# TensorE's issue order taken from the source in the whole program of a two-layer hybrid block

## The chip, the cores and the metric

The kernel runs on one core of one Trainium2 chip. The metric is the device time of one launch in microseconds (us), here the median of the runs shown. A core has TensorE (PE in the profile, its weight loads PEld), VectorE (DVE), ScalarE (ACT), GpSimd (POOL) and SyncE (SP), each with an instruction stream of its own that it works off in order; SP, ScalarE and GpSimd also issue DMAs. An engine waits on semaphores where an instruction needs a result of another engine.

## The reference

Input is `x` (1024 tokens of width 1024), a context of 256 tokens, two conditioning vectors, and the weights of two layers. Each layer does:

```
mod = silu(c) @ ada_w + ada_b                     # six vectors of 1024, for tokens and context
h   = rmsnorm(x) * (1 + scale) + shift            # the same for the context
u   = h @ w_in                                    # split over four mixers of width 256
y   = [rglru(u_a), hgrn2(u_b), ssd(u_s), mla(u_m)]
x   = x + gate * (concat(y) @ w_out)
x   = x + gate * expert_choice_ffn(modulate(rmsnorm(x)))   # 16 experts of width 512
```

`rglru` is a gated linear recurrence after a short convolution, `hgrn2` and `ssd` are chunked linear attentions run forward and backward, `mla` is softmax attention with low-rank projections over context and tokens. Each expert takes the 128 tokens (32 of the context) with the largest router weights for it. The context is carried on to layer 1 and is not updated by it. All is float32.

## The kernel before

**Emission.** Each stage of a layer is a Python generator: `ada` (the modulation vectors), `norm1`, `eproj`, `lru_x`, `lru_gate`, `ssd`, `ssd_chunk`, `ssd_z`, `hgrn_v`, `hgrn_g`, `hgrn_block`, `hgrn_group`, `hgrn_out`, `mla_prep`, `mla` with its `maxima`, `wout`, `route`, `experts`. `layer` (L2024) spawns them as threads, and `weave` (L223) resumes one thread after another, by simple clocks of the engines and by hand-set due times in the table `ORDER`, up to its next `yield`. So the instructions of the stages are emitted woven into one sequence: that is the order of the source. In it, a group of projection matmuls (`proj_ch`, `proj_tok`, in thirds or halves) stands between, say, two levels of a recurrence group.

**Issue.** The compiler does not keep that sequence. It plans each engine by a timing model of its own, takes the emission order as a priority, and lets a later instruction go first on an engine where by its plan the earlier one still lacks an operand or a buffer. It also hands out the buffers of the pools by its plan. The exception is the main part of `experts`, which stands in a region that fixes the order of every engine:

```
L1976        yield from self.wait(f"route{l}.0")
L1977        with self.tc.manual_schedule():
L1978            prep(0)
```

**Matmuls.** Projections split both operands into a high and a low part and make three passes (`ps<-A,W`, `ps<-W,A`, `ps<-C,A` in the profile). `A` holds the activations, `W` weights and small work tiles (7 buffers), `C` (10 buffers) weights and long rows, `M` (14 buffers) short tiles, `ps` the 8 PSUM banks. A plain float32 matmul appears as two records in the trace.

**Places that the prediction speaks of.**
- `ada`, L407: per step of 128 rows of `ada_w` two loads of 512 KB into `W` and four matmuls `ps<-W,sT` of 32 columns of weights. After the first block, which loads into `A`, it is a thread of layer 0 that makes the remaining vectors of both layers.
- `lru_x`, `proj_ch` (L552): projections of the recurrence `rglru`; the weight block is split by ScalarE and VectorE (L530) first.
- `hgrn_group`: level after level, scores (`scores`, L1044, tiles `ps<-C,M`) and, for the two largest levels, blocks added into one bank (L1097, `ps<-C,W`), with products on VectorE (L1100, L1102) between the levels. At most two groups are open at a time.
- `mla_prep`, `first` (L1249): transposes `ps<-cf,W` of a row tile that GpSimd has scaled.
- `ssd` L834 to 836, then `ssd_chunk` L868 and L870: the backward states are finished on VectorE one after another; the chunk's matmuls `ps<-C,C` read them, and the 512-column pair `ps<-W,cf` (L873, L874) follows.
- `place` (L1348): transposes `ps<-cf,M` of a row tile of queries or keys loaded from DRAM.
- `wout` (L1561): the output projection, `ps<-A,W` and `ps<-A,C`.

The profile puts nearly every instruction at L160, the helper through which all are recorded, so its rows are told apart by tiles.

Of the kernel before, what the change touches and what calls it, by code (L numbers as in the profile page):

```python
# [163 lines left out]
class Model:  # L164
# [1891 lines left out]
    def build(self):  # L2056
        self.mod = self.d([2, 2, 6144])
        self.prelude()
        for l in range(self.layers):
            self.layer(l)  # L2060
        if "y" in self.taps:
            for i, w in enumerate("lhs"):
                if w in self.which:
                    o = 0 if self.layers == 1 else 256
                    self.nc.sync.dma_start(self.taps["y"][256 * i:256 * i + 256, o:], self.yT[256 * i:256 * i + 256, o:])
        if "xc" in self.taps:
            self.nc.sync.dma_start(self.taps["xc"], self.xc)
            self.nc.sync.dma_start(self.taps["xl"], self.xl)
# [39 lines left out]
```

## Time and profile before

| | us |
|---|---|
| median of 3 runs | 2840.32 (2839.93 to 2845.86) |
| profiled execution | 2842.43 |
| its span, first to last instruction | 2840.6 |
| TensorE busy, weight loads busy | 2446.1 (86%), 1865.0 |
| VectorE, ScalarE, GpSimd busy | 1910.6, 1181.4, 910.9 |
| mean granted TensorE clock | 0.923 |

Layer 0 runs up to about 1570 us of the span, its expert stage from about 1100; layer 1 follows, with its expert stage from about 2490. Busy time is the time in which at least one instruction of the engine ran. In the rows of the timeline, a line merges neighbouring instructions of one kind: start, length, engine, operation, tiles, count, and in brackets the idle time before it with what ended it.

### The profile page before, as it was taken

The page shows a single profiled execution, that of the slowest core. Times are in us where ns is not written, and L with a number is a line of the kernel's source. Part 1 is how long each engine was busy: PE and PEld are TensorE (multiplying, and loading weights), DVE is VectorE, ACT ScalarE, POOL GpSimd, SP SyncE. Part 2 cuts the span into 40 slices and gives each one's busy share as a digit, 9 for nine tenths or more (in the row PEclk, how much of TensorE's full clock was granted, in tenths as well). Part 3 has the DMA queues.
Part 4 walks back from the last instruction along what each step waited for, and adds up shares of the span by engine and source line. Part 5 has one row for each costly group of instructions (what it writes and reads, how often), then busy time and mean ns, then how long its engine had stood idle before and what let it go on. Part 6 is the DMA issues. An engine that isn't in the chain of part 4 may idle for free. (4 is left out here: it accounts for less than half of the span.)

```text
span 2840.6 us, 50547 instructions
## 1 busy us (share of the span) xinstructions
PE 2446.1 (86%) x19427; PEld 1865.0 (66%) x19427; DVE 1910.6 (67%) x3894; ACT 1181.4 (42%) x2010; POOL 910.9 (32%) x930
## 2 busy tenths in 40 slices
PE   5879999988898794999999599799969989589888
PEld 3658888644554573777777588688746547367776
DVE  5445476566786646677887745753788764699996
ACT  3345223234343112555555352522353442266664
POOL 3112232242531113333333412322444312244443
PEclk8889999999999896999999899889979999789999
DMA  6222226468212433778888411133331034479996
GB/s 249 63 67 62 61 83 188 138 219 296 70 58 97 151 113 132 245 258 290 294 271 279 139 52 37 56 98 98 97 121 40 19 116 137 171 281 357 350 342 217
DMA packets 243440, 455.45 MB, mean 160 GB/s; under 512 B 25688, under 2 KB 155096, under 8 KB 242176
## 3 DMA queue, kind: packets, MB, share of 16 engines
q1 hardware_dynamic: 190176, 365.75, 37.2%
q0 software_dynamic: 12096, 37.75, 5.8%
q10 hardware_dynamic: 40928, 48.72, 4.9%
q8 instruction: 153, 2.51, 0.4%
q14 instruction: 87, 0.71, 0.1%
HBM read 377.55 MB, written 74.60 MB: 159 GB/s over the span
## 5 line engine op out<-in xcount | busy, mean ns | idle before, releaser
L160 PE MATMUL ps<-A,W 128*128 128x512 f32 (+3 forms) x4160 | 965.1, 379 | 34.4 <-ACT W L160 31.5
L160 PEld LDWEIGHTS ps<-A,W 128*128 128x128 f32 x4160 | 739.4, 195 | 179.6 <-ACT W L160 35.4
L160 DVE TENSOR_TENSOR A<-C,A 128x1024 fp32r<-128x1024 f32 x310 | 443.7, 1459 | 93.7 <-ACT A L160 87.4
L160 ACT ACTIVATE M<-ps 128x512 f32<-128x512 f32 (+6 forms) x576 | 262.3, 469 | 525.5 <-PE ps L160 444.3
L160 ACT ACTIVATE A<-C 128x1024 fp32r<-128x1024 f32 x384 | 392.0, 1058 | 187.9 <-DMA C<-in_moe_w_down_dram 64.5
L160 POOL TENSOR_TENSOR A<-C,A 128x1024 fp32r<-128x1024 f32 x74 | 208.0, 2815 | 214.6 <-ACT A L160 161.1
L160 PE MATMUL ps<-W,A 128*128 128x256 f32 x1344 | 192.5, 300 | 8.5 <-DVE A L160 7.4
L160 PE MATMUL ps<-A,M 128*128 128x512 f32 x768 | 186.7, 399 | 0.9 <-ACT M L160 0.9
L160 PEld LDWEIGHTS ps<-W,A 128*128 128x128 f32 x1344 | 177.0, 203 | 11.5 <-DVE A L160 8.1
L160 PE MATMUL ps<-cf,M 128*128 128x128 f32 (+3 forms) x416 | 74.4, 307 | 124.1 <-DVE M L160 89.3
L160 POOL TENSOR_TENSOR C<-C,M 128x512 f32<-128x512 f32 x76 | 110.2, 1461 | 193.9 <-ACT M L160 136.0
L160 PEld LDWEIGHTS ps<-A,M 128*128 128x128 f32 x768 | 142.8, 190 | 36.1 <-issue 3.1
L160 DVE TENSOR_TENSOR C<-C,M 128x512 f32<-128x512 f32 (+2 forms) x196 | 130.1, 676 | 40.7 <-ACT M L160 39.2
L160 PEld LDWEIGHTS ps<-cf,M 128*128 128x128 f32 (+2 forms) x416 | 53.6, 154 | 154.8 <-DVE M L160 74.9
L160 PE MATMUL ps<-C,A 128*32 128x128 f32 (+1 forms) x2528 | 148.0, 290 | 0.0
L160 PE MATMUL ps<-A 96*128 96x512 f32 (+3 forms) x368 | 132.9, 418 | 9.4 <-ACT A L160 4.0
L160 PEld LDWEIGHTS ps<-C,A 128*32 128x32 f32 (+1 forms) x2528 | 134.8, 127 | 6.9 <-issue 4.6
L160 ACT ACTIVATE W<-ps 128x512 fp32r<-128x512 f32 (+2 forms) x156 | 66.0, 476 | 174.8 <-PE ps L160 174.4
L160 PE MATMUL ps<-M,M 128*128 128x64 f32 (+3 forms) x968 | 116.8, 251 | 23.1 <-DVE M L160 12.6
L160 PE MATMUL ps<-A,C 128*128 128x512 f32 x352 | 134.2, 412 | 1.5 <-DVE C L160 1.4
L160 POOL TENSOR_TENSOR W<-W,C 128x512 f32<-128x512 f32 x33 | 49.6, 1521 | 256.9 <-DVE W L160 173.4
L160 ACT ACTIVATE C<-ps 128x512 f32<-128x512 f32 (+4 forms) x116 | 53.9, 469 | 177.8 <-PE ps L160 163.7
(239 smaller groups left out, 3906.7 us busy)
## 6 DMA issues: line engine op xcount, KB each, us to landing
C<-in_moe_w_gate_dram SPq DMA_DIRECT2D x128, 512.0 KB
C<-in_moe_w_up_dram SPq DMA_DIRECT2D x128, 512.0 KB
C<-in_moe_w_down_dram SPq DMA_DIRECT2D x128, 512.0 KB
W<-in_ada_w_dram SPq DMA_DIRECT2D x80, 512.0 KB
W<-in_w_in_dram SPq DMA_DIRECT2D x40, 512.0 KB
C<-dr SPq DMA_DIRECT2D x29, 512.0 KB
dr<-M ACTq DMA_DIRECT2D x114, 128.0 KB
M<-dr SPq DMA_DIRECT2D x46, 256.0 KB
```

Source lines behind the costliest of these rows:

```text
L160: return f(*args, **kw)
```

## The change

The loop over the two layers is put into a region that fixes the issue order of TensorE alone to the order of emission. VectorE, ScalarE, GpSimd and SP are left to the compiler as before, but for the region inside `experts`, which stays and now orders the engines that the outer one does not. `prelude` has no matmul, so every matmul of the program lies in the new region. No instruction, tile or operand is changed.

```
     def build(self):
         self.mod = self.d([2, 2, 6144])
         self.prelude()
-        for l in range(self.layers):
-            self.layer(l)
+        with self.tc.manual_schedule(engines={mybir.EngineType.PE}):
+            for l in range(self.layers):
+                self.layer(l)
```

## Rows read from the trace of the kernel before

**Rows 1.** The page, part 1: busy time, share of the span, instructions.
```profile
PE 2446.1 (86%) x19427; PEld 1865.0 (66%) x19427; DVE 1910.6 (67%) x3894; ACT 1181.4 (42%) x2010; POOL 910.9 (32%) x930
```

**Rows 2.** Busy time by window: length, busy (records) by engine, clock, DMA share, GB/s.
```profile
0.00:228.00 228.00, 168.67 (x961) 124.44 (x962) 108.92 (x188) 94.08 (x142) 59.78 (x72) 0.88 0.35 121
228.00:505.00 277.00, 259.83 (x4124) 235.02 (x4127) 164.06 (x435) 90.92 (x204) 70.96 (x109) 0.96 0.33 101
505.00:907.00 402.00, 362.86 (x1808) 209.00 (x1801) 286.36 (x682) 155.69 (x340) 141.78 (x209) 0.96 0.45 150
907.00:1100.00 193.00, 157.34 (x819) 120.60 (x819) 98.19 (x252) 42.85 (x93) 41.39 (x26) 0.85 0.42 139
1100.00:1570.00 470.00, 421.83 (x4087) 326.50 (x4087) 354.98 (x563) 242.23 (x300) 157.87 (x84) 0.94 0.77 255
1570.00:1985.00 415.00, 353.21 (x4141) 318.01 (x4142) 239.28 (x501) 160.54 (x306) 122.41 (x162) 0.91 0.26 79
1985.00:2350.00 365.00, 316.07 (x1498) 208.19 (x1497) 273.53 (x630) 146.73 (x306) 136.55 (x184) 0.92 0.25 81
...
2500.00:2840.60 340.60, 303.33 (x1444) 244.87 (x1442) 304.55 (x403) 212.59 (x248) 142.99 (x61) 0.96 0.91 318
```

**Rows 3.** Timeline of TensorE, 147 to 168 us, and SyncE's load at 161.
```profile
159.88 3.57 PE L160 MATMUL ps<-A,W 128*128 128x256 f32 x13 [10.99 <-ACT W L160]
163.38 1.37 PE L160 MATMUL ps<-W,sT 128*32 128x512 f32 x4
...
165.59 1.05 PE L160 MATMUL ps<-W,sT 128*32 128x512 f32 x4
...
161.12 0.34 SPq L403 DMA_DIRECT2D W<-in_ada_w_dram  x1
```

**Rows 4.** Timeline of TensorE, 228 to 236 us.
```profile
227.79 2.29 PE L160 MATMUL ps<-A,W 128*128 128x256 f32 x17
232.15 0.46 PE L160 MATMUL ps<-C,M 64*32 64x32 f32 x32 [2.06 <-ACT M L160]
...
233.92 2.36 PE L160 MATMUL ps<-A,W 128*128 128x256 f32 x9
```

**Rows 5.** Timeline of TensorE, 308 to 317 us.
```profile
308.12 1.84 PE L160 MATMUL ps<-W,A 128*128 128x256 f32 x13
311.20 0.62 PE L160 MATMUL ps<-C,W 64*32 64x32 f32 x48 [1.25 <-DVE C L160]
...
313.70 1.02 PE L160 MATMUL ps<-W,A 128*128 128x256 f32 x5
315.05 1.18 PE L160 MATMUL ps<-C,W 64*64 64x64 f32 x24 [0.33 <-DVE C L160]
```

**Rows 6.** Timeline of TensorE and VectorE, 2147.57 to 2154 us.
```profile
2147.57 1.66 PE L160 MATMUL ps<-C,C 64*128 64x128 f32 x9
...
2149.95 2.88 DVE L160 SCALAR_TENSOR_TENSOR C<-C,et 128x64 f32<-128x64 f32 x14
...
2152.03 0.49 PE L160 MATMUL ps<-C,C 64*128 64x128 f32 x4 [0.55 <-DVE C L160]
...
2152.88 0.49 PE L160 MATMUL ps<-C,C 64*128 64x128 f32 x4 [0.35 <-DVE C L160]
```

**Rows 7.** Timeline of TensorE, 2342.13 to 2343 us.
```profile
2342.13 0.63 PE L160 MATMUL ps<-A,W 128*128 128x512 f32 x1
2342.76 0.79 PE L160 MATMUL ps<-A,C 128*128 128x512 f32 x1
```

**Rows 8.** Busy time by window; columns as in rows 2.
```profile
232.30:235.70 3.40, 3.40 (x136) 3.33 (x129) 2.41 (x5) 3.37 (x4) 0.84 (x2) 0.50 0.22 64
```

**Rows 9.** Timeline of TensorE, 564 to 569 us.
```profile
565.35 1.15 PE L160 MATMUL ps<-W,sT 128*32 128x512 f32 x8
566.61 0.68 PE L160 MATMUL ps<-cf,W 128*128 128x128 f32 x3
```

**Rows 10.** Timeline of TensorE, 640 to 656 us.
```profile
652.17 2.77 PE L160 MATMUL ps<-cf,M 128*96 128x128 f32 x12 [4.34 <-DMA M<-dr]
```

## The prediction

> **What bounds the kernel now.** I read the page's first part, then busy time by stretch of the span, then TensorE's own timeline inside the stretches where it issues out of source order. TensorE is busy 86% of the span [rows 1]. By stretch [rows 2] it idles 59.3 us before 228 us, only 17.2 us of 277 between 228 and 505 (gated recurrence groups with projections between them), 39.1 of 402 up to 907 (state-space, attention preparation, attention), 35.7 up to 1100 (output projection, routing), and 48.2 and 37.3 in the two expert stretches. Layer 1 repeats this: 61.8 from 1570 to 1985, 48.9 up to 2350. So between 228 and 505 TensorE itself sets the pace, and elsewhere it often waits for others, who wait for it in turn.
>
> **Which instructions change place.** The program numbers its instructions in the order in which the source emits them, and the trace has them in the order of issue, so the two orders can be set side by side. Of 14,387 matmuls and transposes 2,369 stand elsewhere than in source order, in 56 closed stretches: 2 before 228, 13 from 228 to 505, 19 from there to 907, 3 to 1100, 12 from 1570 to 1985, 7 to 2350. No stretch lies in an expert stage: these stand in source order already, under their own region, so 470 and 340.6 us of the span stay. Nothing is added or removed: the same matmuls, the same bytes, the same work on the other engines. The one change is that where the compiler now lets a later matmul go first because an earlier one lacks its operand, TensorE will stand.
>
> **The cost of one stretch.** Take the state at which the compiler deviates, keep the recorded arrival of each operand, and lay the matmuls end to end in source order.
> - First stretch, 148.9 us [rows 3]. In the source four `ada` matmuls come first (each f32 matmul is two records) and 26 projections behind them. Now 13 projections start at 159.88 after 10.99 us of waiting, and `ada` is put in between, two by two. The second `ada` weight load is issued only at 161.12, so its two matmuls cannot run before about 161.5; they ran at 165.59. In source order all 26 projections stand behind that load: the stretch ends 0.4 us later (landing at 161.5) to 4.5 us later (at 165.6). I take +3.4, a landing near 164.5, nearer to the row in which the matmuls really ran.
> - 308.1 us [rows 5]. In the source 44 matmuls of the recurrence group (32 on tiles of 64*32 and 64*64, then 12 more of 64*64) stand ahead of 18 projections. Now 13 projections fill 308.12 to 309.96 and the group starts at 311.20 after 1.25 us; five more go at 313.70, ahead of the 12, which start at 315.05 after 0.33 us. In source order TensorE waits 311.20 - 308.12 = 3.08 and 315.05 - 313.70 = 1.35: +2.85 us net.
> - 2147.6 us, the largest [rows 6]. The first of the 64*128 matmuls in the source needs the last backward state, of which VectorE is making 14 pieces; it runs at 2152.88. In the source 11 others, the 512-column pair among them, stand behind it; now they start at 2147.57. TensorE would wait 2152.88 - 2147.57 = 5.3 us where it now loses 0.90 (0.55 + 0.35): +4.4.
> - Last stretch, 2342.1 us [rows 7]. One matmul of the output projection is pulled ahead of one that waits for VectorE until 2342.76: +0.6.
>
> The same sum for all 56 stretches, the first and the last of them above: +4.2, +16.5, +18.3, +2.6, +7.6, +7.9, in the order of the list, +57.1 us in all (only one stretch gains, 0.5). Were each operand's arrival fixed, a late TensorE would simply wait less at its next wait, and nearly all would be given back: the lower end is 0. Were each arrival to move with TensorE, all would stay: +57.
>
> Which? From 228 to 505 idle time is 17.2 us, about as much as the 16.5 to be added, and the recurrence is a ping-pong (a level's scores on TensorE, its products on VectorE, the next scores), so arrivals move with TensorE; but two groups are in flight, and a wait of one lets the other get ahead. I let two thirds stay: 11.0. Elsewhere 40.6 us are added beside 36 to 62 us of idle per stretch, so most is taken back: a quarter stays, 10.2.
>
> **The clock.** A wait can also cost after it has ended. At 232.15 TensorE starts again after 2.06 us [rows 4], and the 3.4 us from 232.3 run at a granted 0.50, that is at 1.2 GHz, and not 2.4 [rows 8]: up to 1.7 us more. Source order makes some 12 waits over 2 us where none that long stood: at most 20 us. Many fall among short matmuls or beside a wait that already lowers the clock, and the carry is as above; I take a fifth, 4 us.
>
> Could the engine itself repair the order? While the group's 32 records wait at 232.15, nine projections stand behind them whose eight predecessors in the same accumulation ran by 230.08 (227.79 + 2.29), so that nothing is missing for them; they issue at 233.92, after the group [rows 4]. The Trainium skill, "TensorE: Matmul & The Clock Gate", gives the engine in the table at its head a queue 64 deep with a partial reorder window; were that to let ready matmuls pass a waiting one, the sum would be 0 and not 25. Its Part 3 says that matmuls start and end in program order; the trace agrees, with those nine, so I give the first reading 0.02, inside the "no change" case below.
>
> **Other engines.** ScalarE, VectorE, GpSimd and the DMA queues (SP's loads above all) stay the compiler's outside the expert stages. It plans them against TensorE's plan, so their order shifts too. The bound for one such shift is the worst queue accident in the rows: the projections at 159.88 stood 10.99 us for their weight split on ScalarE [rows 3]. It can come or go: -11 to +11 per accident; I take 0. In 505 to 907 `ada` matmuls are pulled ahead of what the source has first, as at 565.35 ahead of `mla_prep`'s transposes at 566.61 [rows 9]. In source order these run later and hold their two W buffers longer, so their successors' 512 KB loads go out later. Nothing in layer 0 waits for these mods until the output projection; cost 0, at worst another accident of 11.
>
> **Sum.** 11.0 + 10.2 + 4 = +25.2 us. The profiled execution took 2842.43 us (span 2840.60 and 1.83 around it): 2867.6. It lay 2.1 over the median of the runs, 2840.32; on that scale 2865.5.
>
> **Rivals.**
> 1. Taken back (within 0.2%). The filled gaps were slack: every new wait shortens the next. For it: 394.5 us of idle TensorE in the span. Against it: only 17.2 us of that idle lies where 16.5 are added. 2840 + 0 to 5.
> 2. Faster. Place: 505 to 907, 39.1 us idle. There the compiler's filler does harm: `ada` loads of 512 KB crowd the queue, and at 652.17 TensorE stands 4.34 us for an attention operand coming from DRAM [rows 10]; `ada` matmuls held to their source place would let their loads out later, and the chains of attention preparation, chunk and scores would start before the fillers. It decides from the point where those chains, and not TensorE's total, end the stretch. Price: half of the 39.1, -20: 2820. Against it: TensorE is 90% busy there too, and the loads have their source place only later, not fewer.
> 3. Much slower. The compiler's plan of the other engines is upset: three or four accidents of the size of 10.99 us on top of the forecast, in ScalarE's weight splits or SP's loads behind W buffers held longer: 2865 + 35 to 45, about 2905.
>
> **How the numbers follow.** Forecast (slower, +10 to +45) 0.50; rival 3 0.14; rival 1 0.17; rival 2 0.19. A change under 0.2% (5.7 us) can't be told from none here. So faster 0.19, same 0.17, slower 0.64. The likeliest case alone spans 2850 to 2885. The range for 8 in 10 leaves out half of rival 2 below and a part of rival 3 above: 2827 to 2902 (the upper end is close to +57 with some clock).
>
> **What would show it.** Right: TensorE idle from 228 to 505 grows from 17 to about 28 us, with more of its waits ended by VectorE's and ScalarE's tiles; at the twin of 2147 one wait of about 5 us; granted clock a little under 0.923; busy time of all engines and both expert stretches as they are. Wrong by absorption: longer single waits but the same idle per stretch. Wrong by rival 2: 505 to 907 shorter, `ada` later, DMA share lower around 650. Wrong by rival 3: a new single wait of 8 us or more on ScalarE's W tiles or on a load. The forecast as a whole fails if the expert stretches change by more than 2 us, since nothing in it touches them.

## The result, and the profile after

The changed kernel takes 2912.8 us (median of 4 runs, 2901.01 to 2917.27) against 2840.15 for the kernel before in the same comparison (4 runs, 2839.93 to 2845.86): a ratio of 1.0243, 95% interval 1.0219 to 1.0267. It is slower, as forecast, but by 72.6 us and not by 25.2, and it lies above the range's upper end of 2902. The profiled execution took 2911.44 us, with a span of 2909.7.

To know how far two traces of one program differ, the kernel before was profiled a second time (run e5, below); its span is 2839.6. Busy time by window of that second trace, cut at closed places of TensorE's order (the columns are those of [rows 2]):

```profile
0.00:229.10 229.10, 169.83 (x971) 125.63 (x972) 109.30 (x189) 95.13 (x143) 59.74 (x72) 0.88 0.35 120
229.10:505.40 276.30, 258.94 (x4115) 234.17 (x4118) 163.45 (x435) 89.73 (x203) 70.94 (x109) 0.96 0.33 101
505.40:908.70 403.30, 363.55 (x1810) 210.24 (x1807) 287.37 (x683) 155.91 (x340) 141.75 (x209) 0.96 0.45 151
...
1081.80:1596.00 514.20, 433.28 (x4201) 335.44 (x4200) 396.42 (x621) 265.27 (x337) 192.73 (x108) 0.92 0.77 257
1596.00:1978.80 382.80, 346.69 (x4097) 312.03 (x4096) 215.41 (x459) 146.96 (x284) 105.32 (x146) 0.93 0.22 64
1978.80:2344.80 366.00, 317.18 (x1504) 209.18 (x1504) 274.20 (x631) 147.09 (x307) 136.92 (x184) 0.92 0.25 81
...
sum 2839.60, PE 2445.10 PEld 1865.93 DVE 1918.47 ACT 1181.13 POOL 909.13; mean PE 271.68 PEld 207.33 DVE 213.16 ACT 131.24 POOL 101.01
```

The same view of the changed kernel, cut at the same matmuls:

```profile
0.00:234.20 234.20, 174.10 (x969) 126.39 (x969) 109.47 (x189) 95.25 (x144) 59.77 (x72) 0.85 0.35 117
234.20:525.70 291.50, 259.01 (x4115) 237.00 (x4119) 161.23 (x437) 88.49 (x208) 73.13 (x114) 0.94 0.31 94
525.70:960.20 434.50, 368.13 (x1813) 218.35 (x1801) 287.25 (x681) 156.65 (x337) 134.99 (x204) 0.91 0.42 141
...
1133.40:1649.20 515.80, 432.18 (x4201) 335.36 (x4200) 396.17 (x622) 265.16 (x338) 190.09 (x109) 0.92 0.77 256
1649.20:2035.10 385.90, 345.31 (x4095) 310.65 (x4094) 214.28 (x457) 146.93 (x283) 105.53 (x145) 0.94 0.21 63
2035.10:2415.40 380.30, 325.24 (x1507) 216.12 (x1506) 273.99 (x629) 146.41 (x306) 133.72 (x184) 0.88 0.24 76
...
sum 2909.70, PE 2457.33 PEld 1881.97 DVE 1916.49 ACT 1180.59 POOL 901.89; mean PE 273.04 PEld 209.11 DVE 212.94 ACT 131.18 POOL 100.21
```

Read the length and the first number (TensorE busy) of each line; their difference is TensorE's idle time. In all, idle time went from 2839.6 - 2445.1 = 394.5 to 2909.7 - 2457.3 = 452.4 us, +57.9, and busy time grew by 12.2 at the same instructions. By part:

| part (times of before) | longer by | idle | busy | walk of the prediction | idle forecast to stay |
|---|---|---|---|---|---|
| 0 to 229 | 5.1 | +0.8 | +4.3 | 4.2 | 1.0 |
| 229 to 505 | 15.2 | +15.1 | +0.1 | 16.5 | 11.0 |
| 505 to 909 | 31.2 | +26.6 | +4.6 | 18.3 | 4.6 |
| 909 to 1082 | 0.1 | +2.3 | -2.2 | 2.6 | 0.7 |
| 1082 to 1596 (with experts, layer 0) | 1.6 | +2.7 | -1.1 | 0 | 0 |
| 1596 to 1979 | 3.1 | +4.5 | -1.4 | 7.6 | 1.9 |
| 1979 to 2345 | 14.3 | +6.2 | +8.1 | 7.9 | 2.0 |
| rest (with experts, layer 1) | -0.5 | -0.4 | -0.1 | 0 | 0 |
| sum | 70.1 | +57.9 | +12.2 | 57.1 | 21.2 |

So the idle time that came is, in sum, the walk's 57.1 us, of which the forecast let 21.2 stay. That the two sums agree is partly luck: from 505 to 909 us 26.6 came where the walk had 18.3, from 229 to 505 15.1 of 16.5, and in the other four parts that the walk counts 13.8 of 22.3. Before 229 us the loss came as busy time: `ada`'s groups of four records took 1.92 us each, against 1.05 for one of them in [rows 3].

One part of the baseline is uncertain. The first trace of before, e6, e8, e11, e15 and e16, in which TensorE's order from 1596 us on is that of before, are 1.4 to 5.3 us shorter than the second trace from 1596 to 1979, and 0.2 to 3.6 longer from 1979 to 2345. So the +3.1 may be some 6, and the 14.3 some 12.

TensorE's timeline of the changed kernel, at the places of [rows 3 to 6] in that order:

```profile
153.97 1.92 PE L160 MATMUL ps<-W,sT 128*32 128x512 f32 x4 [5.89 <-DMA W<-in_ada_w_dram]
163.78 1.92 PE L160 MATMUL ps<-W,sT 128*32 128x512 f32 x4 [7.89 <-DMA W<-in_ada_w_dram]
...
237.13 0.39 PE L160 MATMUL ps<-C,M 64*32 64x32 f32 x32 [2.95 <-ACT M L160]
...
317.43 0.80 PE L160 MATMUL ps<-C,W 64*32 64x32 f32 x48 [2.76 <-DVE C L160]
319.53 0.72 PE L160 MATMUL ps<-C,W 64*64 64x64 f32 x16 [1.30 <-DVE C L160]
321.27 1.18 PE L160 MATMUL ps<-C,W 64*64 64x64 f32 x24 [1.02 <-DVE C L160]
...
2201.74 2.93 PE L160 MATMUL ps<-C,C 64*128 64x128 f32 x20 [5.14 <-DVE C L160]
```

Where the engine now stands, it stands about as the walk said: 2.76 us at the group of [rows 5] (forecast 3.08), 5.14 at the last backward state of [rows 6] (forecast 5.3). Before the recurrence two waits of 5.89 and 7.89 us for `ada`'s loads replace the 10.99 of [rows 3]; further on two of 4.65 and 2.31 us for such loads, at 201.36 and 205.59, replace one of 7.36 us for a result of VectorE, at 200.58 in the first trace of before.

A wait costs more than itself. Windows of the first trace of before, at the transposes and at the backward states of [rows 6] (clock is the third number from the end):

```profile
541.60:546.00 4.40, 4.40 (x17) 2.81 (x18) 2.04 (x9) 1.59 (x6) 2.02 (x7) 1.00 0.68 181
2147.60:2156.00 8.40, 6.41 (x33) 3.76 (x33) 7.39 (x28) 3.32 (x7) 3.30 (x6) 0.88 0.00 0
```

Windows of the changed kernel right behind two of the new waits, at the same places:

```profile
570.80:575.60 4.80, 4.80 (x16) 4.11 (x17) 0.24 (x1) 0.98 (x4) 2.00 (x7) 0.50 0.13 39
2201.70:2208.20 6.50, 6.46 (x25) 3.89 (x26) 0.67 (x3) 0.00 (x0) 0.00 (x0) 0.53 0.00 0
```

TensorE runs at 1.2 GHz in the first (granted 0.50, against 1.00 before), and at 0.53 behind the second (against 0.88). The mean clock fell from 0.922 to 0.906.

### The profile page after: what moved, and what is told of

Same layout as the page of the kernel before. It is cut to its first block, busy times and chain, and to the rows that moved or that the text cites. A ratio compares the mean times of both kernels' runs of the same rounds, so it can differ in the third digit from the quotient of the medians.

```text
span 2909.7 us, 50539 instructions
## 1 busy us (share of the span) xinstructions
PE 2457.3 (84%) x19427; PEld 1882.0 (65%) x19427; DVE 1916.5 (66%) x3894; ACT 1180.6 (41%) x2010; POOL 901.9 (31%) x930
## 5 line engine op out<-in xcount | busy, mean ns | idle before, releaser
L160 PE MATMUL ps<-A,W 128*128 128x512 f32 (+3 forms) x4160 | 970.8, 381 | 20.6 <-ACT W L160 16.6
```

The costliest lines, as they stand in the source:

```text
L160: return f(*args, **kw)
```

## The experiments

Two means fix an order in part. Stamping a matmul puts it into source order among the stamped ones; by tiles and shapes the traces of e1, e2, e8 and e11 have the stamped matmuls in the changed kernel's order. Chains of order-only edges from a list (`PINNED`) fix any order of any engine. The buffers of the pools are dealt out by the compiler in each case. The numbers of parts in the expectations are counted from the starts of weight loads and lie up to 1 us beside the table above. Differences are against the runs of before that stood beside each group (2845.05, 2843.26, 2844.71, 2848.10).

**e1. Source order in layer 1 alone.**

```
+        if Meter.seen > 8400:      # matmuls of layer 1, by rank in the source
+            Meter.tc.stamp_issue_order_token(r.ins, "pe")
```

> TensorE's order is fixed to the source in layer 1 only. Three theories go through all the runs. Carry: every wait that TensorE makes in source order stays in the time, because the work it then releases late is what it waits for next; nothing is given back. Replanning: the other engines' order, which the compiler plans anew beside TensorE's new order, makes the loss. Held buffers: `ada` matmuls at their source place hold W buffers longer, and SyncE's loads, the ones of other stages too, stand behind them. In the changed kernel TensorE's time from 1570 us on grew by 25.8 us (6.9 + 13.6 + 0.9 + 4.4), while the walk with fixed arrivals gave 7.6 + 7.9 = 15.5. Carry, and held buffers too, since layer 1 has no `ada`: 2840 + 15 to 26, that is 2855 to 2866, and the first 1570 us as before. The forecast's own quarter would give 2840 + 4 to 6. If the loss of layer 1 is inherited from layer 0's lateness: 2840 within 3.

2866.45 us, +21.4 (ratio 1.0070, 1.0047 to 1.0092). Layer 1's loss is its own and not inherited from layer 0.

**e2. All but `ada` in source order.**

```
+        if not inside("ada"):
+            Meter.tc.stamp_issue_order_token(r.ins, "pe")
```

> All of TensorE's instructions but the `ada` matmuls are in source order; `ada` is left to the compiler. The walk with fixed arrivals gives 46.3 us for the order that comes out of it, against 57.1 for the whole change (3.5 less before 228 us, 7.2 less from 505 to 907). Carry: 2840 + 46 to 62, that is 2886 to 2902, with most of the new idle from 505 to 907 still there. Held buffers: the +32.2 us from 505 to 907 and the +5.3 before 228 go nearly whole, so 2912 - 30 to 37 = 2876 to 2883, and the 6.06 us wait of `mla_prep`'s transposes at 570.8 us is not there. Replanning: no number of its own.

2888.55 us, +43.5 (1.0152, 1.0130 to 1.0174). The part from 505 to 909 us is 13.7 us longer than before and not 31.2; the wait at 570.8 us is gone. 29 of the 72.6 us hang on the place of 192 of 14,387 matmuls, more than the walk's 10.8 for them.

**e3. The orders crossed.**

```
+PINNED = {"PE": order of before, "Activation": order of after, "DVE": ..., "Pool": ..., "SP": ...}
```

> The orders are crossed: TensorE issues exactly in the order of the kernel before, and ScalarE, VectorE, GpSimd and SyncE issue exactly in the order that the compiler gave them in the changed kernel (209, 441, 85 and 87 of their instructions stand elsewhere than before). Carry and held buffers: the loss is TensorE's order, so 2840 within 6. Replanning: the loss comes along with the other engines' order, 2840 + 20 to 72.

2878.57 us, +33.5 (1.0110, 1.0087 to 1.0132): within the range of replanning (20 to 72), and not the 6 us at most of carry and held buffers. The other engines' new order is no neutral thing under TensorE's old one: 505 to 909 us got 20.6 us longer, 1979 to 2345 12.3.

**e4. Fifty stretches in source order, every other engine in the order of before.**

```
+PINNED = {"PE": order of before with 50 of its 56 stretches sorted by source, others: order of before}
```

> TensorE is in source order in 50 of the 56 stretches and in the order of before in the other six; every other engine issues exactly in the order of the kernel before. The walk with fixed arrivals gives 49.4 us for these 50 (4.2, 12.1, 15.2, 2.6, 7.3, 7.9 in the six parts outside the expert stages). Carry: 2840 + 49 to 60, with the idle of TensorE growing in every part by about its term. The forecast's shares (two thirds from 228 to 505, a quarter elsewhere, 4 for the clock) would give 8.1 + 9.3 + 4 = 21: 2861. Replanning: as little as the forecast or less, 2840 to 2861, since no other engine's order is changed. Held buffers: from 505 to 907 more than its 15.2.

2919.95 us, +74.9 (1.0259, 1.0237 to 1.0281): as much as the whole change, without a single instruction of another engine in a new place. So the loss can come without replanning. That the two sums are equal is luck, though. From 505 to 909 us e4 is 56.5 us longer, for a walk of 15.2, where the whole change is 31.2 longer; the other five parts grew by 21.3 us together, for a walk of 34.1, where they grew by 37.8 in the whole change. The compiler's new order for the other engines is thus a remedy from 505 to 909 at most; under TensorE's old order (e3) it made that same part longer, so the orders fit each other in pairs. Window of that part:

```profile
516.40:976.20 459.80, 378.09 (x1810) 219.69 (x1809) 287.90 (x683) 155.24 (x340) 137.38 (x209) 0.87 0.40 132
```

Idle is 81.7 us where it was 39.8; 15.03 us of it are one wait for a weight split of ScalarE, at 664.12, which neither kernel has. In the other five parts the lengths grew by 3.3, 7.7, -0.6, -0.3 and 11.2 us (walk 4.2, 12.1, 2.6, 7.3, 7.9). So carry's "every part by about its term" fails from 909 to 1082, and against the second trace from 1596 to 1979 too. SyncE's stand for buffers shows here: its waits at `mla_prep`'s row loads (L1242) that a matmul of TensorE ended (us in total, times, longest), in the first trace of before from 505 to 700 us and in e4 from 516 to 735:

```profile
SPq L1242 <- PE ps L160: 15.1, 7, 3.4
SPq L1242 <- PE ps L160: 59.4, 5, 19.8
```

**e5. The kernel before once more.** No edit.

> The kernel before once more, for a second trace of it: how far two traces of one program differ part by part. So far every kernel tried, also the one with only layer 1 changed, spent 4 to 5 us more of TensorE's time in the expert stage of layer 1 than the first trace of before, and 3 to 9 less in that of layer 0. If the first trace was a low draw there, this one shows the same +4 and the parts differ by up to 5 us either way; if the parts agree within 1 us, those differences belong to the changes.

2841.39 us. The expert stage of layer 0 is 10.0 us shorter than in the first trace of before, that of layer 1 4.9 longer and 1596 to 1979 3.3 longer; all other parts agree within 0.9 us. So the first trace was a draw, and so is the second: the expert stage of layer 0 is 1.1 to 16.5 us longer than there in the other kernels' traces (16.5 in e16, at 530.7), though none of them touches it. The changed kernel's +1.6 and -0.5 against the second trace lie within that. Other parts that a kernel leaves alone vary by up to 5.5 us (505 to 909 in e1).

**e6. Only `ada` at its source place.**

```
+PINNED = {"PE": order of before, the 192 matmuls of ada moved behind all that the source has ahead of them}
```

> The other half of the run with `ada` free: only the 192 `ada` matmuls are put at their source place (right behind whatever in the order of before covers all that the source has ahead of them), all other matmuls keep the order of before among themselves; the other engines are left to the compiler. The walk with fixed arrivals gives 20.3 us (4.2 before 228 us, 1.9 to 505, 14.2 from 505 to 907). The run with `ada` free was 43.5 us over before, the whole change 72.6, so if the two halves add up this one is 2840 + 29. Held buffers: 2866 to 2875, most of it from 505 to 907, with transposes of `mla_prep` waiting some 6 us behind a load of SyncE. Carry: 2840 + 20, the walk's own sum. The forecast's view (nothing waits for these vectors, so it costs nothing): 2840 within 5.

2874.02 us, +30.8 (1.0115, 1.0083 to 1.0147); with e2 this makes 74.3 of 72.6. From 505 to 909 it is 26.4 us longer, of a walk of 14.2, and `mla_prep`'s transposes wait 5.30 us at 554.27. The forecast's "cost 0" for `ada` fails here.

**e7. `ada`'s loads issued by GpSimd.**

```
-                    nc.sync.dma_start(w, wk[k][:, c0:c0 + 1024])
+                    nc.gpsimd.dma_start(w, wk[k][:, c0:c0 + 1024])
```

> The changed kernel, but the loads of `ada_w` after the first block are issued by GpSimd and not by SyncE. TensorE's order is that of the changed kernel to the last matmul. Held buffers: a load that waits for a W buffer no longer keeps SyncE from issuing the loads behind it, so the 6.06 us wait at 570.8 us and most of the excess from 505 to 907 over the walk (26.4 - 18.3 = 8 us of idle, 5.6 of busy time) go: 2912 - 8 to 18, that is 2894 to 2904. Against it: GpSimd, 32% busy, waits for the buffers in SyncE's place, and what it adds and scales comes late: 2912 or more. Carry: SyncE's queue is not what counts, 2912 within 5.

2921.44 us, +78.2 (1.0275, 1.0248 to 1.0303). The 6.06 us wait is gone, but waits of 6.38 (first row tile) and 5.28 us (`ada`) have come ahead of it: GpSimd now stands for the buffers. It does not tell the queue from the buffers.

**e8. Source order from 505 us to the experts of layer 0 alone.**

```
+        if 3510 < Meter.seen <= 5500:
+            Meter.tc.stamp_issue_order_token(r.ins, "pe")
```

> TensorE in source order only for the matmuls that the source has between rank 3510 and the expert stage of layer 0 (505 to 1100 us of before); the rest, and all other engines, left to the compiler. The walk with fixed arrivals gives 20.9 us (18.3 and 2.6). In the changed kernel these parts grew by 32.2 and shrank by 0.6. If a stretch's loss is its own and not inherited from the stretches ahead: +26 to +34 here, 2866 to 2875. Carry at its walk: 2861. The forecast's quarter: 2846.

2873.28 us, +30.0 (1.0110, 1.0084 to 1.0137), the part itself +32.0: the same as within the whole change, and kept to the end.

**e9 and e10. `ada` neither waits nor holds, in both kernels.**

```
-                nc.tensor.matmul(pm[...], self.sT[:, k, :], ws[g // 2][:, 512 * (g % 2):...],
+                nc.tensor.matmul(pm[...], self.sT[:, k, :], (ws[g // 2][:, 512 * (g % 2):...] if first else dg(self.cf, 0, [[0, 4], [1, 128]])),
```

> The changed kernel with the same loads of `ada_w` into the same W buffers, but the `ada` matmuls after the first block multiply by a resident constant block and not by what was loaded, so they wait for no load and hold no buffer, and the modulation vectors are not the reference's. TensorE's order is that of the changed kernel to the last matmul. Held buffers: the waits that end with `mla_prep`'s matmuls from 505 to 907 fall from 18.4 us (changed kernel) to about the 7.6 of before, `ada`'s own 10.7 to nearly none; 2912 - 20 to 30, that is 2882 to 2892. Carry at the walk: only `ada`'s own waits go, 2912 - 8 to 12, and `mla_prep` still waits some 18 us.

> The same edit in the kernel before, as the partner of the last run: `ada` matmuls with a constant operand, loads unchanged, the order of all engines left to the compiler. The trace of before has 8.3 us of waits that end with `ada` matmuls from 505 to 907; the compiler, free to put them anywhere, may save these: 2830 to 2840. The difference of the last run to this one is what source order costs when `ada` neither waits nor holds: held buffers 43 to 50 us (as with `ada` free), carry at the walk 57 to 72.

2856.36 us in the changed kernel (+11.7; 1.0050, 1.0024 to 1.0075), 2832.60 in the one before (-12.1; 0.9970, 0.9953 to 0.9986): the pair is then 23.8 us apart and not 72.6. That is below every number given. It isn't the price of source order without `ada`, though. In e10 the compiler planned TensorE's order anew (3479 of its 19,427 records stand elsewhere than in before), and some 18 of the 24 us by which the two traces differ arise behind 1082 us, most of them in layer 1, which has no `ada`. The part from 505 to 909 is 409.2 us long, 25.3 less than in the changed kernel, and before 229 us 30.5 and 28.2 us went, in the one kernel and the other. In the changed kernel 27.4 us of waiting for `ada`'s loads stood there, in the one before 6.8, beside waits for ScalarE's and VectorE's tiles. Of e10's 28.2 us only 19.5 are left at 505 us and 12.1 at the end: here later waits did take a difference back. The waits of TensorE from 505 to 909, summed by what ended them (us in total, times, longest), in the second trace of before:

```profile
PE ps L160 <- POOL W L160: 2.9, 2, 1.8
```

In the changed kernel:

```profile
PE ps L160 <- POOL W L160: 13.2, 6, 6.1
```

In e9:

```profile
PE ps L160 <- POOL W L160: 6.8, 6, 1.8
```

These are the row tiles of `mla_prep` that GpSimd scales: with `ada` letting go of the buffers 6.4 of the 10.3 us of new waiting are gone, and the longest single wait is that of before. Of the 26.6 us of new idle time from 505 to 909, 14.3 are still there. Waits that end with any matmul of `mla_prep` fell only from 18.4 to 14.0, so the expected return to 7.6 was wrong.

**e11. Source order from 228 to 505 us alone.**

```
+        if 853 < Meter.seen <= 3510:
+            Meter.tc.stamp_issue_order_token(r.ins, "pe")
```

> TensorE in source order only for the matmuls that the source has from rank 853 to 3510 (228 to 505 us of before), all else left to the compiler. The walk with fixed arrivals gives 17.5 us (16.5 and 1.0 behind it). In the changed kernel this part grew by 14.4 us against the second trace of before. If a part keeps its loss to the end of the program: 2841 + 12 to 18, 2853 to 2859, with the parts behind it as before within 4 us. Forecast's two thirds: 2852. If later waits take it back: 2841 within 5.

2860.93 us, +16.2 (1.0054, 1.0037 to 1.0072); the part itself +14.7, TensorE idle 32.2 us where it was 17.4. All of it is kept to the end.

**e12. One stretch, eleven matmuls.**

```
+PINNED = {"PE": order of before with the stretch at 2147.6 us sorted by source, others: order of before}
```

> Only the one stretch at 2147.6 us is put into source order: 11 matmuls change place, all other instructions of all engines issue in the order of before. The walk gives +4.40 us. Carry: TensorE's idle from 1985 to 2350 us grows by 4 to 5 us in this trace and the time by as much, 2841 + 4. The forecast's quarter: idle there +1, 2842. Later waits of the same part shrink in turn, if at all, within 100 us behind it.

2849.05 us, +4.3 (1.0018, 0.9999 to 1.0036), too little to be timed, but not to be seen in the trace. Timeline of TensorE in the second trace of before:

```profile
2124.28 3.57 PE L160 MATMUL ps<-cf,nm 128*1 128x128 f32 x16 [2.88 <-DVE nm L160]
...
2145.34 0.49 PE L160 MATMUL ps<-C,C 64*128 64x128 f32 x4 [0.56 <-DVE C L160]
2146.19 0.49 PE L160 MATMUL ps<-C,C 64*128 64x128 f32 x4 [0.35 <-DVE C L160]
2147.76 3.35 PE L160 MATMUL ps<-cf,nm 128*1 128x128 f32 x16 [1.08 <-DVE nm L160]
...
2197.95 1.91 PE L160 MATMUL ps<-cf,nm 128*1 128x128 f32 x16 [1.72 <-DVE nm L160]
...
2317.92 1.22 PE L160 MATMUL ps<-A,W 128*128 128x512 f32 x2 [8.47 <-ACT W L160]
```

The same matmuls in e12:

```profile
2122.00 3.57 PE L160 MATMUL ps<-cf,nm 128*1 128x128 f32 x16 [2.86 <-DVE nm L160]
...
2143.84 2.93 PE L160 MATMUL ps<-C,C 64*128 64x128 f32 x20 [5.13 <-DVE C L160]
2146.70 2.81 PE L160 MATMUL ps<-W,cf 128*128 128x512 f32 x4
2152.47 3.23 PE L160 MATMUL ps<-cf,nm 128*1 128x128 f32 x16 [2.97 <-DVE nm L160]
...
2202.57 1.91 PE L160 MATMUL ps<-cf,nm 128*1 128x128 f32 x16 [1.71 <-DVE nm L160]
...
2322.52 1.22 PE L160 MATMUL ps<-A,W 128*128 128x512 f32 x2 [8.48 <-ACT W L160]
```

Ahead of the stretch e12 is 2.28 us early (2122.00 against 2124.28), behind it 4.62 late (2202.57 against 2197.95): it cost 6.9 us, for a walk of 4.40; the wait right behind it grew too, from 1.08 to 2.97 us. And 120 us later the offset is 4.60: the long wait there is 8.48 us as it was 8.47, and that of 1.72 is 1.71. Nothing of this stretch is taken back. What ends those waits is made from earlier results of TensorE (row maxima of its scores; the mixers' outputs, which `wout` loads and splits) and is late by as much.

**e13 and e15. `mla_prep`'s row loads issued by GpSimd, in both kernels.**

```
-            nc.sync.dma_start(u, umd[128 * t:128 * t + 128, :])
+            nc.gpsimd.dma_start(u, umd[128 * t:128 * t + 128, :])
```

> The changed kernel, but `mla_prep`'s row loads (L1242) are issued by GpSimd, which scales the same rows next, and not by SyncE. TensorE's order is that of the changed kernel. Queue (the row loads are late because they stand in SyncE's queue behind `ada` loads that wait for a W buffer and behind stores that wait for VectorE): `mla_prep`'s waits from 505 to 907 fall from 18.4 to 8 to 11 us and the time by 8 to 12: 2900 to 2905. Buffers (the rows themselves are W tiles and wait for one whoever loads them): within 4 us of 2912, `mla_prep` still waits 16 or more. GpSimd in SyncE's place: its own work comes late, 2915 or more.

> The partner of the run with the row loads on GpSimd: the same edit in the kernel before. There `mla_prep` waits only 7.6 us from 505 to 907, some 1.8 of it at the first row tile: little to gain. Queue: 2836 to 2843, so the difference between the partners shrinks from 72 to about 62. Otherwise the difference stays at 70.

2917.50 us (+69.4; 1.0242, 1.0218 to 1.0267) and 2850.40 (+2.3; 1.0012, 1.0000 to 1.0024): the difference between the partners stays, at 67.1. `mla_prep` waits 18.2 us.

**e14 and e16. `mla_prep`'s stores issued by ScalarE, in both kernels.**

```
-                nc.sync.dma_start(qkd[1, T, :], qt.rearrange("p h e -> p (h e)"))
-            nc.sync.dma_start(qkd[0, T, :], kt.rearrange("p h e -> p (h e)"))
+                nc.scalar.dma_start(qkd[1, T, :], qt.rearrange("p h e -> p (h e)"))
+            nc.scalar.dma_start(qkd[0, T, :], kt.rearrange("p h e -> p (h e)"))
```

> The changed kernel, but `mla_prep`'s stores of finished rows (L1296, L1297) are issued by ScalarE and not by SyncE; TensorE's order is that of the changed kernel. SyncE waited some 64 us in these stores between 525 and 735 us of the changed kernel, against 39 in the same part of before. Queue: the loads behind them go out when their buffers are free, `mla_prep`'s and part of the others' waits go, 2912 - 8 to 20: 2892 to 2904. Buffers: within 4 us of 2912. ScalarE now waits for VectorE in these stores and what it splits and copies comes late: 2916 or more.

> The partner of the run with the stores on ScalarE: the same edit in the kernel before; TensorE's order is that of before but for 15 places. Queue: SyncE waits 39 us less in stores, loads go out earlier, 2830 to 2841, and the difference between the partners falls by as much as the changed kernel gains more. If ScalarE is held up by the stores: 2845 to 2855.

2917.14 us (+69.0; 1.0255, 1.0237 to 1.0272) and 2850.44 (+2.3; 1.0015, 1.0000 to 1.0030), a difference of 66.7. `mla_prep` still waits 18.2 us. Neither edit brings the gain, but they don't acquit the order in which SyncE issues: e14 leaves the row loads in it, and in e13 GpSimd issues them behind its own work. Timeline of TensorE, GpSimd and SyncE in the changed kernel:

```profile
554.63 6.72 SPq L403 DMA_DIRECT2D W<-in_ada_w_dram  x3
...
560.06 1.05 PE L160 MATMUL ps<-W,sT 128*32 128x512 f32 x4 [1.97 <-DMA W<-in_ada_w_dram]
561.33 1.05 PE L160 MATMUL ps<-W,sT 128*32 128x512 f32 x4 [0.22 <-DMA W<-in_ada_w_dram]
562.32 2.42 PE L160 MATMUL ps<-A,W 128*128 128x256 f32 x18
...
563.99 0.46 POOL L160 TENSOR_TENSOR M<-M,wr 128x128 f32<-128x128 f32 x1 [5.28 <-DVE s L160]
564.47 0.33 SPq L1296 DMA_DIRECT2D dr<-M  x1
564.89 0.39 SPq L1528 DMA_DIRECT2D wr<-in_moe_router_dram  x1
565.37 0.64 SPq L403 DMA_DIRECT2D W<-in_ada_w_dram  x1
566.10 0.38 SPq L1242 DMA_DIRECT2D W<-dr  x1
570.79 0.90 PE L160 MATMUL ps<-cf,W 128*128 128x128 f32 x3 [6.06 <-POOL W L160]
```

In the first trace of before the row load stood ahead of that store and went out while the projections ran: SyncE had waited 1.5 us for a matmul of TensorE, and the load went out 0.05 us after `ada`'s four records of 537.20 had ended:

```profile
537.20 1.05 PE L160 MATMUL ps<-W,sT 128*32 128x512 f32 x4
538.18 2.17 PE L160 MATMUL ps<-A,W 128*128 128x256 f32 x16
538.30 3.41 SPq L1242 DMA_DIRECT2D W<-dr  x2
...
541.59 0.68 PE L160 MATMUL ps<-cf,W 128*128 128x128 f32 x3 [0.24 <-POOL W L160]
```

So in before it is a buffer that lets the row load go. In the changed kernel it isn't: `ada`'s last matmul of that group ends at 562.38, and the row load goes out at 566.10 without a wait of its own. What keeps it is SyncE's order: a store (L1296) that waits until 564.47 for a product of GpSimd, which had itself waited 5.28 us for VectorE, and two other loads stand ahead. Six projections that belong to the same accumulation as the 18 at 562.32, and whose operands were complete at 561.0, stand behind the transposes for the 6.06 us. In e13 the same row load goes out at 565.39, behind a memset of GpSimd that ends at 565.18, and the transposes still wait 2.99 us; in e14 SyncE stands at the load L1528 until 566.06 instead, the row load goes out at 567.29, and the wait is 5.43. How `ada`'s place comes to make these waits stays open: the buffers are seen at work in before and in e4, an issue order at the longest wait of the changed kernel. No run puts the row loads ahead of that store, or gives the row tiles a pair of buffers of their own.

## Why the prediction was right and wrong

- *The direction and the mechanism* were right: ready matmuls behind one that waits, most of them in layer 0, with the sizes of the single waits as worked out ([rows 5, 6]). The walk's sum, +57.1, is the idle time that came, +57.9.
- *The failed step is the share that stays*: "elsewhere ... most is taken back: a quarter stays, 10.2". Without 229 to 505, the walk had 40.6 and 42.8 came (57.9 - 15.1): 26.6 for 18.3 from 505 to 909, where a quarter would be 4.6, and 13.8 for 22.3 in the other walked parts, where a quarter would be 5.6. The reason given, that 36 to 62 us of idle per stretch would absorb it, took idle time for slack. e12 shows that at its stretch it is none: two later waits kept their lengths to 0.01 us, and the lateness was still there 120 us on. From 229 to 505, where two thirds (11.0) were to stay, 15.1 did, and e11 shows them kept to the end. It is no law: e10 gave part of its gain back, and in e4 909 to 1082 lost nothing of a walk of 2.6.
- *"Nothing in layer 0 waits for these mods ...; cost 0"* is the second failed step, and part of the first. Indeed nothing waits for its result, but e2, e6 and e9 show that its place decides most of 505 to 909 (26.4 us alone, where the forecast had 4.6 for the whole part). The W buffers, which the prediction names in the sentence before, have a share: in e9, where `ada` doesn't hold them, 6.4 of the 10.3 us of new waits for GpSimd's tiles are gone. The path in the changed kernel stays open, since at its longest such wait SyncE stood in a store and not for a buffer. The size is not fully settled: of e9's gain of 25.3 us in that part 12.4 are idle and 12.9 busy time (9.3 of these in the `ada` matmuls themselves, 44.2 to 34.9), and no run shows the reason of the latter.
- *The clock*, taken as a fifth of 20 us, 4: busy time grew by 12.2 at the same instructions. The single price was right (0.50 behind a wait), the share too small. Part of it, above all the 8.1 from 1979 to 2345, is not separable: e8 changed nothing there and is 3.6 us longer.
- *Other engines*, "I take 0": e4 shows that the loss comes without their new order, and e3 that this order costs 33.5 us under TensorE's old one. The two can't be priced one by one.
- *The expert stages*, unchanged within 2 us: +1.6 and -0.5 against the second trace, -8.4 and +4.4 against the first. The stage of layer 0 varies by up to 16.5 us in kernels that leave it alone, so this sign could not decide anything.
- *The rivals.* In sum nothing was taken back (rival 1), though single parts kept less than their walk. 505 to 909 got longer, not shorter (rival 2): `ada` did move behind the transposes that it preceded in [rows 9] (613.56 and 599.12 us now), and the operand wait of [rows 10] is 3.19 us instead of 4.34, but that is 1 us against 31. Rival 3's 2905 is nearest, but no new wait is 8 us long (the longest is 7.89): the loss is 57 us in many waits and not three or four accidents. Its "SP's loads behind W buffers held longer" is seen in e4; at the 6.06 us wait of the changed kernel SP's load stood behind a store.
- *The engine does not mend the order*, as the six ready projections behind the transposes show. The Trainium skill, "TensorE: Matmul & The Clock Gate", Part 3, "The mechanism", says that matmuls start and end strictly in the order of issue; the trace agrees, and were it otherwise, the 6.06 us would have been filled.

## What to carry to other kernels

Idle time of an engine is slack only if what ends it does not depend on that engine: follow the next long waits behind a delay back to their source, and if it is the same engine, expect the delay to stay. When an instruction is moved later, price what it keeps waiting as well as its result: here 192 matmuls whose result nothing in the layer waited for cost 30.8 us by their place alone. Before you blame a buffer for a late load, look at what stands ahead of that load in the order of the engine that issues it. And take a second trace of the kernel before, since parts that nothing touched can differ by 5 us, and a stage with heavy weight traffic by up to 16.5.

## What the runs showed of the hardware

- The expert stage of layer 0 differed by 10.0 us between two traces of one program (524.2 and 514.2 us), at 0.77 of the DMA engines' time, while every stage without heavy weight traffic but one repeated within 0.9 us. In e16, which leaves that stage alone, it took 530.7 us.
- After a wait of 5 to 6 us TensorE ran at a granted 0.50 to 0.53 for the 4.8 to 6.5 us that were looked at.
- SyncE worked off its issues in order: a row load stood until 566.10 us behind a store that waited until 564.47 for a product of GpSimd, and behind two other loads.
